# Gate products, decay sums and operand differences moved to VectorE, and mixer B started with its values

## The chip, the cores and the metric

The kernel runs on one core of one Trainium2 chip. The metric is the time on the device in microseconds (us). The kernel before takes 2028.79 us as the median of three runs (2027.69 to 2029.82).

A core has five engines with a queue of instructions each, worked off in order: TensorE (PE in the profile, its weight loads PEld), VectorE (DVE), ScalarE (ACT), GpSimd (POOL) and SyncE (SP), which here only starts transfers (DMA). An instruction that has to wait for another engine holds up everything behind it in its own queue.

## What is computed

The reference has two layers on a sequence of 512 tokens with 2048 features.

```
x: (1, 512, 2048) float32
# layer 1, mixer A (16 heads of 128)
h = rmsnorm(x);  q, fz, i, gate = split(h @ a_w_in)
log_f = logaddexp(log(lb), log1p(-lb) + log_sigmoid(fz))
k = (1 - lb) * sigmoid(-fz)
o = hgrn2_chunkwise(q, k, i, log_f)        # gated linear recurrence in chunks
x = x + (head_rmsnorm(o) * silu(gate)) @ a_w_out
# layer 2, mixer B (16 heads of 128)
h = rmsnorm(x);  k, v, f = split(h @ kv_w);  F = cumsum(log_sigmoid(f + bias))
q, gate = split(h' @ b_w_in)               # h' has its own norm weights
p = softmax(causal(head_rmsnorm(q) . head_rmsnorm(k) / sqrt(128) + F[t] - F[s]))
x = x + (head_rmsnorm(p @ v) * silu(gate)) @ b_w_out
```

`lb` is the lower bound of the forget gate, one number for each feature of the keys.

## The kernel before

Everything is kept with features on the 128 partitions and the 512 tokens along the free dimension: the stream is 16 tiles of 128 x 512. Each float32 operand of a large product is split in two (`split`, L439: a cast to a high part on ScalarE, L440, and the subtraction that gives the low part on VectorE, L441), and each product is made of three matmuls: high by high, high by low and low by high.

**Groups.** `group` (L220) is one pass over the 16 tiles of the stream with 512 output features in four PSUM banks, 192 matmuls of 512 columns. Its weights come from `Chunks` (L168): a transfer of 512 KB on SP's queue brings the weights of two steps into one of two `wr` buffers, and they are split into one of three `wh`, `wl` pairs. Where norm weights go into the weights, the split scales them (L147, L148), and for a group with two sets of scales it does so in two halves. Results are taken from the banks by an `evac` function: `qf_evac` (L544), `qk_evac` (L893), `v_evac` (L414) and `gate_evac` (L379).

**Mixers.** The order of the groups is written out by hand: `order_a` for mixer A, `order_b` for mixer B, with `q` for two heads of queries and keys (or forget inputs), `v` for four heads of values and `g` for the gates of four heads. After each `q` group two heads are added to a list of tasks, `mix_a` or `mix_b`, written as generators; `pump` takes steps from the list between the steps of the following groups, two a step in mixer A and one a step in mixer B. In mixer A GpSimd makes the logarithm of the decay (L568) and the small sums of it (L611 to L613, L661 to L663, L717, L718).

**Output projections.** `out_product` finishes all tasks, opens a new pool of buffers, and makes the first 512 features with a plain `group`, whose `before` splits the branch output (`y_split`) and, at every second step, prepares the operands for the rest (`quick_prep`, L254). The other 1536 features are six groups (`quick`, L270) in which a 2 x 2 block product takes seven products of half the columns in place of eight; the operand sums `m` of the stream come from `quick_prep`, those of the weights from `w_sums` (L153). Both take their buffers from the same two of the name `wm`. `w7h` and `w7l` are the split weights, in two buffers. `quick_sum` (L300) puts the products together and adds the residual, which a transfer has brought into one of four `z` buffers. The first projection's result `X1` is stored (`x1_done`, L809) for the residual of the second one, and kept. Its last quick group is only put together two steps into the first group of mixer B (`last_a`).

**Start of mixer B.** The first group of mixer B runs `x1_split` (L850) ahead of each of its 16 steps. It splits one tile of `X1` and adds its squares to a running sum (`norm1.add`, L349: a square on ScalarE, L354, into a `z` buffer, and a sum on VectorE, L355). After the last step the sum is finished, and the forget gate's product (`forget`) follows.

**The order on each engine.** The framework sorts the instructions of all engines by a timeline that it makes from its own costs, with the order of the program as priority; so the order in an engine's queue is fixed when the kernel is built, and it is not always that of the lines. Waits between engines are set by the framework from what each instruction reads and writes.

Of the kernel before, what the change touches and what calls it, by code (L numbers as in the profile page):

```python
# [12 lines left out]
AF = mybir.ActivationFunctionType  # L13
ALU = mybir.AluOpType
AX = mybir.AxisListType

P = 128
# [3 lines left out]
H = 16  # L21
# [5 lines left out]
RATE_A, RATE_B = 2, 1  # L27
# [5 lines left out]
def hgrn2_fox(ctx, tc, io):  # L33
# [24 lines left out]
    def const(tag, shape, dt=F32):  # L58
        return padded(cp, shape, dt, tag, tag)
# [108 lines left out]
    class Chunks:  # L168
# [33 lines left out]
        def split(self):  # L202
            if self.raw:
                fn, _ = self.raw.pop(0)
                self.parts.extend(fn())
# [47 lines left out]

    def quick_prep(p, y):  # L254

        k1, k2 = 2 * p, 2 * p + 1
        b11, b12, b21, b22 = y[k1][:, :TN], y[k1][:, TN:], y[k2][:, :TN], y[k2][:, TN:]
        m = mt("wm", (P, 4, TN), 2)
        V.tensor_sub(m[:, 0, :], b12, b11)
        G.tensor_sub(m[:, 2, :], b12, b22)  # L260
        V.tensor_sub(m[:, 1, :], b22, m[:, 0, :])
        V.tensor_sub(m[:, 3, :], b21, m[:, 1, :])
        th = mt(f"th{p}", (P, 3, TN), 1, F32R)
        tl = mt(f"tl{p}", (P, 3, TN), 1, F32R)
        split(m[:, 0, :], Xh[k1][:, TN:], Xl[k1][:, TN:])
        split(m[:, 1:4, :], th, tl)
        return th, tl

    def quick(banks, prep, evac, hold):

        half = lambda i: banks[i // 2][:, (i % 2) * TN : (i % 2 + 1) * TN]
        for p in range(KT // 2):
            if p % 2 == 0:
                wts.load()
            if not wts.parts:
                wts.split()
            h, l = wts.take()
            if not (wts.parts or hold and p == KT // 2 - 1):
                wts.split()
            th, tl = prep[p]  # L280
            k1, k2 = 2 * p, 2 * p + 1
            lo, hi = slice(0, TN), slice(TN, T)
            f, e = p == 0, p == KT // 2 - 1

            for i, (a, xh, xl) in enumerate((
                (2, Xh[k1][:, lo], Xl[k1][:, lo]),
                (5, th[:, 0, :], tl[:, 0, :]),
                (1, th[:, 2, :], tl[:, 2, :]),
                (3, Xh[k1][:, hi], Xl[k1][:, hi]),
                (0, Xh[k2][:, lo], Xl[k2][:, lo]),  # L290
                (6, Xh[k2][:, hi], Xl[k2][:, hi]),
                (4, th[:, 1, :], tl[:, 1, :]),
            )):
                o = half(i)
                PE.matmul(o, h[:, a, :], xh, start=f and i % 2 == 0, stop=False)
                PE.matmul(o, h[:, a, :], xl, start=False, stop=False)  # L296
                PE.matmul(o, l[:, a, :], xh, start=False, stop=e and (i % 2 == 1 or i == 6))
        return lambda: evac(*banks)
# [71 lines left out]
    def log_sigmoid(out, z, l):  # L370

        S.activation(l, z, AF.Abs)
        S.activation(l, l, AF.Exp, scale=-1.0)
        S.activation(l, l, AF.Ln, bias=1.0)
        V.scalar_tensor_tensor(out, z, 0.0, l, op0=ALU.min, op1=ALU.subtract)
# [3 lines left out]
    def gate_evac(norm, h0):  # L379
        def evac(j, bk):  # L380
            h = h0 + j
            new = Y[h] is None
            if new:
                Y[h] = nt(f"y{h}", (P, T), 1)
            z = Y[h] if new else nt("z", (P, T), 4)
            V.tensor_mul(z, bk, norm.row)
            l = tmp()
            log_sigmoid(l, z, l)
            S.activation(l, l, AF.Exp)
            G.tensor_mul(z, z, l)  # L390
            if not new:
                V.tensor_mul(Y[h], Y[h], z)

        return evac
# [92 lines left out]
    lb = const("lbv", (P, H))  # L487
    one_m = const("one_m", (P, H))
    log_lb = const("log_lb", (P, H))
    log_1m = const("log_1m", (P, H))  # L490
    diff = const("diff", (P, H))

    def lower_bounds():
        lbl = vec["lb"]
        V.tensor_sub(lb, lbl, lbl)
        S.activation(lb, lb, AF.Exp)
        V.reciprocal(one_m, lb)
        V.tensor_mul(lb, lb, one_m)
        V.tensor_sub(lb, lb, lb)
        S.activation(log_1m, lb, AF.Ln, scale=-1.0, bias=1.0)  # L500
        V.tensor_scalar(out=log_lb, in0=lb, scalar1=2.0**-60, scalar2=None, op0=ALU.max)
        S.activation(log_lb, log_lb, AF.Ln)
        V.tensor_scalar(out=one_m, in0=lb, scalar1=0.0, scalar2=NEG, op0=ALU.is_le, op1=ALU.mult)
        V.tensor_add(log_lb, log_lb, one_m)
        V.tensor_sub(diff, log_1m, log_lb)

    setup.append(lower_bounds)

# [35 lines left out]
    def qf_evac(h0):  # L544
        def evac(j, bk):
            h = h0 + j // 2
            need("qk", h - 3)
            need("g", h - 2)
            if j % 2 == 0:
                QA[h] = mt("q", (P, T), 3)  # L550
                V.tensor_mul(QA[h], bk, norm0.row)  # L551
                return
            z = nt("z", (P, T), 4)
            V.tensor_mul(z, bk, norm0.row)
            ls, l = tmp(), tmp()
            log_sigmoid(ls, z, l)
            V.scalar_tensor_tensor(l, z, 0.0, l, op0=ALU.max, op1=ALU.add)
            KA[h] = mt("k", (P, T), 3)
            b1 = log_1m[:, h : h + 1]
            S.activation(KA[h], l, AF.Exp, scale=-1.0, bias=b1)  # L560
            S.activation(l, ls, AF.Abs, bias=diff[:, h : h + 1])
            S.activation(l, l, AF.Exp, scale=-1.0)
            S.activation(l, l, AF.Ln, bias=1.0)
            V.tensor_scalar(
                out=ls, in0=ls, scalar1=b1, scalar2=log_lb[:, h : h + 1], op0=ALU.add, op1=ALU.max
            )
            GA[h] = mt("g", (P, T), 2)
            G.tensor_add(GA[h], ls, l)  # L568

        return evac  # L570

# [220 lines left out]
    norm1 = Norm()  # L792
    X1 = [None] * KT

    order_b = "q0 v0 q1 q2 v1 g0 q3 q4 v2 g1 q5 q6 v3 q7 g2 g3".split()
    nb, nk = vec["b_norm_w"], vec["kv_norm_w"]
    for name in order_b:
        ap = io[{"q": "wb_qk", "v": "wb_v", "g": "wb_g"}[name[0]]][int(name[1])]
# [9 lines left out]

    def x1_done(kt):  # L809
        nc.sync.dma_start(x1_d[kt], X1[kt])  # L810

    def out_a_evac():
        res = [res_a(j) for j in range(4)]
# [15 lines left out]
    def out_product(evac0, residual, evac, name, hold):  # L829

        flush()
        phase(name)
        prep = []

        def before(kt):
            y_split(kt)
            if kt % 2:
                prep.append(quick_prep(kt // 2, Yd))

        group(evac0, before=before)  # L840
        return quick_groups(prep, residual, evac, hold)
# [8 lines left out]
    def x1_split(kt):  # L850
        if kt == 2:
            last_a()
        if kt == 6:
            forget_weights()
        h, l = new_x(kt)
        split(X1[kt], h, l)
        norm1.add(X1[kt])
        X1[kt] = None
        if kt == KT - 1:
            norm1.finish()  # L860
# [14 lines left out]
    def forget():  # L875
        b = bank()
        for kt in range(KT):
            PE.matmul(b[0:48], wfs[:, kt, :], Xh[kt], start=kt == 0, stop=False)
            PE.matmul(b[0:48], wfs[:, kt, :], Xl[kt], start=False, stop=kt == KT - 1)
        z = nt("z", (P, T), 4)  # L880
        S.copy(z[0:H], b[32 : 32 + H])
        V.tensor_add(z[0:H], z[0:H], b[0:H])
        V.tensor_mul(z[0:H], z[0:H], norm1.row[0:H])
        V.tensor_scalar(out=z[0:H], in0=z[0:H], scalar1=vec["f_bias"], scalar2=None, op0=ALU.add)
        l = tmp()
        log_sigmoid(l[0:H], z[0:H], l[0:H])
        f = tmp()
        V.tensor_tensor_scan(f[0:H], l[0:H], l[0:H], initial=0.0, op0=ALU.add, op1=ALU.bypass)
        nc.sync.dma_start(f_d, f[0:H])
# [3 lines left out]
    def qk_evac(h0):  # L893
        def evac(j, bk):
            h = h0 + j % 2
            need("qk", h - 3)
            t = mt("q" if j < 2 else "k", (P, T), 3)
            (QB if j < 2 else KB)[h] = t
            V.tensor_mul(t, bk, norm1.row)

        return evac
# [78 lines left out]

    reached.clear()
    VV[:] = [None] * H
    first = True
    for name in order_b:
        kind, i = name[0], int(name[1])
        if kind == "q":
            group(qk_evac(2 * i), before=x1_split if first else None, rate=RATE_B)
            if first:
                forget()
            first = False  # L990
            tasks.append((2 * i, mix_b(2 * i)))
            tasks.append((2 * i + 1, mix_b(2 * i + 1)))
        elif kind == "v":
            group(v_evac(norm1, 4 * i), token_major=True, rate=RATE_B)
        else:
            group(gate_evac(norm1, 4 * i), rate=RATE_B, hold=name == order_b[-1])

    def res_b(kt):
        r = nt("z", (P, T), 4)
# [96 lines left out]
```

## Time and profile before

| | us |
|---|---|
| median of 3 runs | 2028.79 |
| profiled execution | 2028.22 |
| its span, first to last instruction | 2026.5 |
| TensorE busy | 1985.9 |
| VectorE busy | 1567.6 |
| ScalarE busy | 1129.0 |
| GpSimd busy | 271.9 |

The span is that of one execution, the rest of its time lies around it. In the rows of the profile, `out<-in` are the names of the tiles, `x1664` is a count, and the number in square brackets of a timeline row is how long the engine was idle just before it and what ended that. In groups of instructions, the first number after the bar is the busy time in us and the second the mean of one in ns. Instructions of one engine overlap at their ends, so that a row of 0.68 us can follow the one before it after 0.60.

Mixer A runs to about 860 us, the first output projection to about 1045, mixer B to about 1845, and the second projection to the end.

### The profile page before, as it was taken

To read this page: it belongs to the slowest core of one execution; us is meant where nothing else is said; L and a number is where in the kernel's file an instruction comes from. 1 tells how busy PE (TensorE), PEld (TensorE's weight loads), DVE (VectorE), ACT (ScalarE), POOL (GpSimd) and SP (SyncE) were. 2 spreads that over 40 slices of the span, in tenths; PEclk is the share of its full clock that TensorE was granted. 3 is DMA by queue.
4 is the path that set the end of the run, shared out by engine and by line. 5 is a ranking of instruction groups with operands and counts; after the bars stand their busy time and mean duration, and the time that the engine had idled before them with its cause. 6 is when DMAs were issued, how large, how long until landed. Compare 5 with 4: busy or idle time off the path is not lost.

```text
span 2026.5 us, 28907 instructions
## 1 busy us (share of the span) xinstructions
PE 1985.9 (98%) x10218; PEld 1697.4 (84%) x10218; DVE 1567.6 (77%) x3271; ACT 1129.0 (56%) x2312; POOL 271.9 (13%) x365
## 2 busy tenths in 40 slices
PE   9999999999999999989989999999999999999898
PEld 7888888888888888869977888888888888888898
DVE  7969977989799889798884667666766676687887
ACT  6646655666566466653363655554555556565432
POOL 3303211312133041130000000010001000012100
PEclk9999999999999999999999999999999999999899
DMA  5222222222222222335432232223223322323453
GB/s 188 83 84 73 73 84 83 74 81 76 80 78 70 77 84 73 94 113 166 151 99 91 92 95 92 88 81 104 92 80 97 96 86 87 91 81 107 138 162 104
DMA packets 61697, 195.02 MB, mean 96 GB/s; under 512 B 7904, under 2 KB 8032, under 8 KB 61552
## 3 DMA queue, kind: packets, MB, share of 16 engines
q1 hardware_dynamic: 61408, 193.17, 30.7%
q8 instruction: 80, 1.31, 0.3%
q14 instruction: 65, 0.53, 0.1%
q10 hardware_dynamic: 144, 0.01, 0.0%
HBM read 184.73 MB, written 8.42 MB: 95 GB/s over the span
## 4 chain that ended last, share of the span: by engine, by line
PE 71%; DVE 14%; DMA 6%; issue 3%; ACT 3%; POOL 3%; SPq 0%; DVEq 0%; ACTq 0%; POOLq 0%
PE gm L242 15%; PE gm L244 15%; PE gm L243 15%; PE gm L239 5%; PE gm L238 5%; PE gm L240 5%; DMA wr<-in_wb_q 3%; DVE wl L441 2%; DMA wr<-in_wa_q 2%; DVE w7l L441 2%; PE mx L587 1%; PE mx L585 1%; PE mx L586 1%; DVE ml L441 1%; PE mx L435 1%
## 5 line engine op out<-in xcount | busy, mean ns | idle before, releaser
L242 PE MATMUL gm<-xh,wh 128*128 128x512 f32 x1664 | 650.9, 392 | 4.0 <-ACT t L304 1.7
L243 PE MATMUL gm<-xl,wh 128*128 128x512 f32 x1664 | 650.2, 391 | 0.0
L244 PE MATMUL gm<-xh,wl 128*128 128x512 f32 x1664 | 613.2, 392 | 4.4 <-DVE wl L441 3.9
L242 PEld LDWEIGHTS gm<-xh,wh 128*128 128x128 f32 x1664 | 313.1, 188 | 68.6 <-ACT t L304 1.9
L244 PEld LDWEIGHTS gm<-xh,wl 128*128 128x128 f32 x1664 | 310.8, 188 | 69.6 <-DVE wl L441 7.2
L243 PEld LDWEIGHTS gm<-xl,wh 128*128 128x128 f32 x1664 | 313.1, 188 | 62.8
L441 DVE TENSOR_TENSOR wl<-wr,wh 128x512 fp32r<-128x512 f32 x288 | 213.2, 744 | 67.7 <-ACT wh L440 57.8
L440 ACT CAST wh<-wr 128x512 fp32r<-128x512 f32 x288 | 177.2, 619 | 124.1 <-PE gm L243 89.8
L148 DVE SCALAR_TENSOR_TENSOR wl<-wr,v_b_norm_w,wh 128x256 fp32r<-128x256 f32 (+1 forms) x192 | 113.1, 591 | 139.8 <-ACT wh L147 130.7
L147 ACT ACTIVATE wh<-wr,v_b_norm_w 128x256 fp32r<-128x256 f32 (+1 forms) x192 | 111.7, 585 | 186.2 <-PE gm L243 146.7
L239 PE MATMUL gm<-wl,xh 128*128 128x512 f32 x512 | 201.6, 394 | 0.4 <-DVE wl L441 0.4
L240 PE MATMUL gm<-wh,xl 128*128 128x512 f32 x512 | 199.9, 391 | 0.0
L238 PE MATMUL gm<-wh,xh 128*128 128x512 f32 x512 | 183.8, 392 | 0.3 <-DVE q L551 0.2
L147 ACT ACTIVATE wh<-wr,v_kv_norm_w 128x256 fp32r<-128x256 f32 (+1 forms) x192 | 110.3, 574 | 59.5 <-PE gm L240 43.2
L148 DVE SCALAR_TENSOR_TENSOR wl<-wr,v_kv_norm_w,wh 128x256 fp32r<-128x256 f32 (+1 forms) x192 | 111.2, 581 | 35.8 <-ACT wh L147 35.3
L938 POOL TENSOR_SCALAR_AFFINE_SELECT s<-s 128x128 f32<-128x128 f32 x64 | 27.4, 428 | 804.1 <-DVE s L937 803.5
L580 DVE COPY_PREDICATED at<-masks,mx 128x128 f32<-128x128 uint8 (+3 forms) x448 | 106.8, 297 | 11.2 <-PE mx L587 10.7
L238 PEld LDWEIGHTS gm<-wh,xh 128*128 128x128 f32 x512 | 96.0, 188 | 20.5 <-ACT wh L440 0.5
L239 PEld LDWEIGHTS gm<-wl,xh 128*128 128x128 f32 x512 | 96.3, 188 | 19.3 <-DVE wl L441 1.0
L240 PEld LDWEIGHTS gm<-wh,xl 128*128 128x128 f32 x512 | 96.3, 188 | 18.4
L440 ACT CAST w7h<-wr 128x768 fp32r<-128x768 f32 x48 | 40.1, 835 | 110.1 <-PE mx L296 45.3
L440 ACT CAST kh<-k 128x512 fp32r<-128x512 f32 (+1 forms) x96 | 56.4, 587 | 52.4 <-PE mx L586 19.4
(221 smaller groups left out, 3948.4 us busy)
## 6 DMA issues: line engine op xcount, KB each, us to landing
wr<-in_wb_qk SPq DMA_DIRECT2D x64, 512.0 KB, 3.5
wr<-in_wa_qf SPq DMA_DIRECT2D x62, 512.0 KB, 3.5
wr<-in_wa_v SPq DMA_DIRECT2D x32, 512.0 KB, 3.5
wr<-in_wa_g SPq DMA_DIRECT2D x32, 512.0 KB, 3.5
wr<-in_wb_v SPq DMA_DIRECT2D x32, 512.0 KB, 3.5
wr<-in_wb_g SPq DMA_DIRECT2D x32, 512.0 KB, 3.5
wr<-in_wa_q SPq DMA_DIRECT2D x24, 512.0 KB, 3.5
wr<-in_wb_q SPq DMA_DIRECT2D x24, 512.0 KB, 3.6
```

The lines of the kernel that those rows point to most:

```text
L147: S.activation(h[:, c], r[:, c], AF.Copy, scale=w[:, kt : kt + 1])
L148: V.scalar_tensor_tensor(l[:, c], r[:, c], w[:, kt : kt + 1], rd(h)[:, c], op0=ALU.mult, op1=ALU.subtract)
L238: PE.matmul(banks[j], xh, h, start=f, stop=False)
L239: PE.matmul(banks[j], xh, l, start=False, stop=False)
L240: PE.matmul(banks[j], xl, h, start=False, stop=e)
L242: PE.matmul(banks[j], h[:, c], Xh[kt], start=f, stop=False)
L243: PE.matmul(banks[j], h[:, c], Xl[kt], start=False, stop=False)
L244: PE.matmul(banks[j], l[:, c], Xh[kt], start=False, stop=e)
L440: S.copy(h, src)
L441: return V.tensor_sub(l, src, rd(h))
L580: V.copy_predicated(out, mv, data)
L938: G.affine_select(out=s[:, c], in_=s[:, c], pattern=[[-1, P]], compare_op=ALU.is_ge, fill=NEG, base=0, channel_multiplier=1,)
```

## The change

- In `gate_evac` the product of a gate's input with its sigmoid goes from GpSimd to VectorE.
- In `qf_evac` the factor 1 - lb goes into the logarithm (`Ln` of `c1 * e + c1` with `c1 = 1 / (1 - lb)`), so that `ls` holds the log sigmoid with log(1 - lb) already added; the sum that gives the log decay, on GpSimd before and with a VectorE step ahead of it, is one VectorE instruction. The setup makes `inv_1m` and `neg_lb` in place of `log_1m` and `diff`.
- In `quick_prep` one difference goes from GpSimd to VectorE, and the split of the first difference into `Xh`, `Xl` comes after the split of the other three; it is returned as a function, which `before` calls at once.
- `norm1.add` goes from `x1_split` to `x1_done`.
- Mixer B's order starts with `v0` and then `q0`; the first group, now `v0`, runs `x1_split` and is followed by `forget`.

The small sums of mixer A and the causal selection in mixer B (L938) stay on GpSimd.

```diff
     def quick_prep(p, y):
...
         V.tensor_sub(m[:, 0, :], b12, b11)
-        G.tensor_sub(m[:, 2, :], b12, b22)
+        V.tensor_sub(m[:, 2, :], b12, b22)
         V.tensor_sub(m[:, 1, :], b22, m[:, 0, :])
         V.tensor_sub(m[:, 3, :], b21, m[:, 1, :])
...
-        split(m[:, 0, :], Xh[k1][:, TN:], Xl[k1][:, TN:])
         split(m[:, 1:4, :], th, tl)
-        return th, tl
+        return th, tl, lambda: split(m[:, 0, :], Xh[k1][:, TN:], Xl[k1][:, TN:])
...
-            G.tensor_mul(z, z, l)
+            V.tensor_mul(z, z, l)
...
-        S.activation(log_1m, lb, AF.Ln, scale=-1.0, bias=1.0)
+        V.tensor_scalar(out=inv_1m, in0=lb, scalar1=-1.0, scalar2=1.0, op0=ALU.mult, op1=ALU.add)
+        V.reciprocal(inv_1m, inv_1m)
...
-        V.tensor_sub(diff, log_1m, log_lb)
+        V.tensor_scalar(out=neg_lb, in0=log_lb, scalar1=-1.0, scalar2=None, op0=ALU.mult)
...
-            log_sigmoid(ls, z, l)
+            c1, c2 = inv_1m[:, h : h + 1], log_lb[:, h : h + 1]
+            S.activation(l, z, AF.Abs)
+            S.activation(l, l, AF.Exp, scale=-1.0)
+            S.activation(l, l, AF.Ln, scale=c1, bias=c1)
+            V.scalar_tensor_tensor(ls, z, 0.0, l, op0=ALU.min, op1=ALU.subtract)
             V.scalar_tensor_tensor(l, z, 0.0, l, op0=ALU.max, op1=ALU.add)
...
-            S.activation(KA[h], l, AF.Exp, scale=-1.0, bias=b1)
-            S.activation(l, ls, AF.Abs, bias=diff[:, h : h + 1])
+            S.activation(KA[h], l, AF.Exp, scale=-1.0)
+            S.activation(l, ls, AF.Abs, bias=neg_lb[:, h : h + 1])
...
-            V.tensor_scalar(
-                out=ls, in0=ls, scalar1=b1, scalar2=log_lb[:, h : h + 1], op0=ALU.add, op1=ALU.max
-            )
-            G.tensor_add(GA[h], ls, l)
+            V.scalar_tensor_tensor(GA[h], ls, c2, l, op0=ALU.max, op1=ALU.add)
...
-    order_b = "q0 v0 q1 q2 v1 g0 q3 q4 v2 g1 q5 q6 v3 q7 g2 g3".split()
+    order_b = "v0 q0 q1 q2 v1 g0 q3 q4 v2 g1 q5 q6 v3 q7 g2 g3".split()
...
     def x1_done(kt):
         nc.sync.dma_start(x1_d[kt], X1[kt])
+        norm1.add(X1[kt])
...
                 prep.append(quick_prep(kt // 2, Yd))
+                prep[-1][2]()
...
         split(X1[kt], h, l)
-        norm1.add(X1[kt])
         X1[kt] = None
```

More of the change, by code (lines that the diff above doesn't have):

```diff
@@ L279, in quick @@
                 wts.split()
-            th, tl = prep[p]
+            th, tl, _ = prep[p]
             k1, k2 = 2 * p, 2 * p + 1
@@ L489, in hgrn2_fox @@
     log_lb = const("log_lb", (P, H))
-    log_1m = const("log_1m", (P, H))
-    diff = const("diff", (P, H))
+    neg_lb = const("neg_lb", (P, H))
+    inv_1m = const("inv_1m", (P, H))
     def lower_bounds():
@@ L555, in evac @@
             ls, l = tmp(), tmp()
-            log_sigmoid(ls, z, l)
+            c1, c2 = inv_1m[:, h : h + 1], log_lb[:, h : h + 1]
[3 more added lines that the diff above has]
+            V.scalar_tensor_tensor(ls, z, 0.0, l, op0=ALU.min, op1=ALU.subtract)
             V.scalar_tensor_tensor(l, z, 0.0, l, op0=ALU.max, op1=ALU.add)
             KA[h] = mt("k", (P, T), 3)
-            b1 = log_1m[:, h : h + 1]
-            S.activation(KA[h], l, AF.Exp, scale=-1.0, bias=b1)
-            S.activation(l, ls, AF.Abs, bias=diff[:, h : h + 1])
+            S.activation(KA[h], l, AF.Exp, scale=-1.0)
+            S.activation(l, ls, AF.Abs, bias=neg_lb[:, h : h + 1])
             S.activation(l, l, AF.Exp, scale=-1.0)
             S.activation(l, l, AF.Ln, bias=1.0)
-            V.tensor_scalar(
-                out=ls, in0=ls, scalar1=b1, scalar2=log_lb[:, h : h + 1], op0=ALU.add, op1=ALU.max
-            )
             GA[h] = mt("g", (P, T), 2)
-            G.tensor_add(GA[h], ls, l)
+            V.scalar_tensor_tensor(GA[h], ls, c2, l, op0=ALU.max, op1=ALU.add)
         return evac
@@ L982, in hgrn2_fox @@
     VV[:] = [None] * H
-    first = True
     for name in order_b:
         kind, i = name[0], int(name[1])
+        before = x1_split if name == order_b[0] else None
         if kind == "q":
[L987 to L990, printed above, removed]
+            group(qk_evac(2 * i), before=before, rate=RATE_B)
             tasks.append((2 * i, mix_b(2 * i)))
@@ L993, in hgrn2_fox @@
         elif kind == "v":
-            group(v_evac(norm1, 4 * i), token_major=True, rate=RATE_B)
+            group(v_evac(norm1, 4 * i), token_major=True, before=before, rate=RATE_B)
         else:
             group(gate_evac(norm1, 4 * i), rate=RATE_B, hold=name == order_b[-1])
+        if before:
+            forget()
     def res_b(kt):
```

## The prediction

> **What bounds the kernel now.** The order of reading was the first part of the page, then the busy time by stretches, then TensorE's own waits in the timeline.
>
> ```profile
> PE 1985.9 (98%) x10218; PEld 1697.4 (84%) x10218; DVE 1567.6 (77%) x3271; ACT 1129.0 (56%) x2312; POOL 271.9 (13%) x365
> 200.00:250.00 50.00, 49.15 (x245) 41.49 (x244) 49.08 (x126) 34.16 (x77) 10.91 (x15) 1.00 0.24 73
> 905.00:920.00 15.00, 9.56 (x59) 9.27 (x60) 11.50 (x19) 5.55 (x7) 0.00 (x0) 0.77 0.65 214
> 925.00:1015.00 90.00, 89.80 (x749) 89.60 (x748) 74.02 (x116) 35.69 (x41) 0.00 (x0) 1.00 0.48 153
> 1015.00:1055.00 40.00, 31.79 (x195) 28.55 (x194) 39.07 (x68) 25.95 (x49) 0.00 (x0) 0.91 0.24 83
> 1890.00:1905.00 15.00, 9.73 (x54) 9.43 (x54) 11.27 (x19) 4.95 (x7) 0.00 (x0) 0.66 0.65 211
> ```
>
> In the stretches the columns are the length, then busy time of PE, weight load, DVE, ACT and POOL, the granted clock, DMA share and GB/s. TensorE is busy for 98% and the change takes no matmul from it, so only its gaps can be won. They are bunched: at the start of the first output projection (905 to 920), at the start of mixer B (1015 to 1055) and at the start of the second output projection (1890 to 1905). In each the granted clock falls too: 15 x 0.23 = 3.45 us, 40 x 0.09 = 3.6 us and 15 x 0.34 = 5.1 us of full clock are lost. The waits themselves, in the PE timeline:
>
> ```profile
> 908.78 0.39 PE L295 MATMUL mx<-th,w7h 128*128 128x256 f32 x1 [4.04 <-ACT w7h L440]
> 912.17 0.58 PE L297 MATMUL mx<-th,w7l 128*128 128x256 f32 x1 [1.66 <-DVE w7l L441]
> ...
> 1025.85 0.39 PE L297 MATMUL gm<-xh,w7l 128*128 128x256 f32 x1 [1.20 <-DVE w7l L441]
> ...
> 1035.21 0.39 PE L295 MATMUL gm<-th,w7h 128*128 128x256 f32 x1 [3.39 <-ACT w7h L440]
> ...
> 1037.87 0.58 PE L297 MATMUL gm<-th,w7l 128*128 128x256 f32 x1 [0.81 <-DVE w7l L441]
> ...
> 1044.76 0.50 PE L242 MATMUL gm<-xh,wh 128*128 128x512 f32 x1 [1.68 <-ACT t L304]
> ...
> 1894.35 0.58 PE L295 MATMUL mx<-th,w7h 128*128 128x256 f32 x1 [4.34 <-ACT w7h L440]
> ...
> 1897.36 0.58 PE L297 MATMUL mx<-th,w7l 128*128 128x256 f32 x1 [0.93 <-DVE w7l L441]
> ```
>
> With the clock this makes 4.04 + 1.66 + 3.45 = 9.2 us, 1.20 + 3.39 + 0.81 + 1.68 + 3.6 = 10.7 us and 4.34 + 0.93 + 5.1 = 10.4 us: 30.3 us, all of it behind operands of the seven-product groups (`w7h`, `w7l`) that ScalarE and VectorE finish late. Mixer A adds one more group, from the waits of PE:
>
> ```profile
> PE mx L585 <- ACT mh L440: 4.9, 4, 1.6
> ```
>
> That is 4.9 us in four waits. Some 35 us in all is the most that can be won.
>
> **The change part by part: the two output projections.** Four gate products (L390) and eight differences (L260) leave GpSimd at each. What they do now, from the timelines of POOL, DVE and ACT at the first one:
>
> ```profile
> 863.82 6.36 POOL L390 TENSOR_TENSOR z<-z,t 128x512 f32<-128x512 f32 x4 [22.40 <-ACT t L389]
> 896.32 4.42 POOL L260 TENSOR_TENSOR wm<-y,y 128x256 f32<-128x256 f32 x2 [4.45 <-DVE tl L441]
> ...
> 862.15 0.69 DVE L375 SCALAR_TENSOR_TENSOR t<-z,t 128x512 f32<-128x512 f32 x1 [0.35 <-ACT t L374]
> ...
> 865.59 1.77 DVE L392 TENSOR_TENSOR y<-y,z 128x512 f32<-128x512 f32 x1
> 867.29 3.44 DVE L441 TENSOR_TENSOR wl<-wr,wh 128x512 fp32r<-128x512 f32 x2
> ...
> 872.95 0.68 DVE L392 TENSOR_TENSOR y<-y,z 128x512 f32<-128x512 f32 x1
> 875.36 0.75 DVE L259 TENSOR_TENSOR wm<-y 128x256 f32<-128x256 f32 x2
> ...
> 876.63 1.28 DVE L441 TENSOR_TENSOR wl<-wr,wh 128x512 fp32r<-128x512 f32 x2
> ...
> 900.06 0.96 DVE L261 TENSOR_TENSOR wm<-y,wm 128x256 f32<-128x256 f32 x1
> 900.95 0.41 DVE L262 TENSOR_TENSOR wm<-y,wm 128x256 f32<-128x256 f32 x1
> ...
> 907.23 0.42 DVE L158 TENSOR_TENSOR wm<-wm,wr 128x256 f32<-128x256 f32 x1
> ...
> 905.49 0.83 ACT L440 CAST w7h<-wr 128x768 fp32r<-128x768 f32 x1 [1.94 <-DMA wr<-in_wa_q]
> ...
> 907.68 1.04 ACT L440 CAST w7h<-wm 128x1024 fp32r<-128x1024 f32 x1 [1.05 <-DVE wm L158]
> ```
>
> The reader sees two costs of GpSimd. Its result is late: the last pair of L260 runs from 896.32 to 900.74 and L262 follows at 900.95. And VectorE is slowed beside it: the same L392 takes 1.77 us beside L390 and 0.68 after it, two `wl` 3.44 against 1.28, one L261 0.96 against the 0.41 of L262. The two `wm` buffers tie the rest together: L158, for the first weights of the quick groups, comes only after the operand sums have been split, and the cast of 907.68, which ends PE's wait, after L158.
>
> On VectorE the gates cost 4 x 0.61 = 2.4 us (0.68 with overlap: the two `wl` above step by 0.60) and the differences 8 x 0.34 = 2.7 us (L259 takes 0.75 for two, so 0.34 a step). Taken away are (1.77 - 0.68) + (3.44 - 1.28) + (0.96 - 0.41) = 3.8 us in the rows shown. So VectorE's work is close to even, and the bounds of this term are a chain 5.1 - 3.8 = 1.3 us later, if VectorE alone sets it, and one 4.42 - 0.75 + 3.8 - 2.4 = 5.1 us earlier, if the last pair's stay on POOL and the whole relief at the gates count. I take 3 us earlier, nearer the upper end, since the last gate result no longer waits for four products in a row and L262 no longer for POOL. The wait of 4.04 then falls to 1.0. Waits of 1.66 and 1.68 are not followed by a lower clock in the stretches, those of 3.39, 4.04 and 4.34 are, so the 3.45 us goes too: **6.5 us**. The second projection has the same shape: 4.34 falls to 1.3 and 5.1 us of clock returns: **8.1 us**. What is late next is the second weight chunk: its cast (905.49) waited for a load, and loads follow the `wl` splits.
>
> [...]
>
> The plain order inside `quick_prep` changes as well: the sums are cast and split before the first difference overwrites half of `Xh`. No instruction is added; the deferred part is called at once in the same step, so nothing leaves the plain group's loop. I count it at zero, between 0 and 0.41 us a pair (the step of one short instruction). Its cover is that the split half is read only by the quick groups.
>
> **The start of mixer B.** The 15 squares and sums of the norm move from here into the first projection.
>
> ```profile
> 1015.00:1055.00 40.00, 10.22 (x15) 0.91 0.24 83
> ...
> 1033.66 0.41 DVE L158 TENSOR_TENSOR wm<-wm,wr 128x256 f32<-128x256 f32 x1
> ...
> 1044.14 0.57 ACT L304 COPY t<-gm 128x512 f32<-128x512 f32 x1
> ...
> 1023.04 0.68 DVE L355 TENSOR_TENSOR rstd<-rstd,z 128x512 f32<-128x512 f32 x1
> ...
> 1032.27 0.68 DVE L355 TENSOR_TENSOR rstd<-rstd,z 128x512 f32<-128x512 f32 x1
> ```
>
> The first row is the stretch with L355 alone: 10.22 of the 39.07 us in which VectorE is full. Three of them (the first and the last shown, one between) stand ahead of L158 in its queue: 3 x 0.61 = 1.8 us. The 3.39 falls to 1.6, the clock (3.6) returns, and the copy L304, which stood behind squares on ScalarE, starts about 1.0 us earlier, for **6.4 us**; bounds 0 (the planner fills the freed places with splits of `X1`) and 10.7. Starting with `v0` adds no matmul; its weights are split whole and not in two halves, and the row totals of this stretch leave that under 1 us, counted at zero. Its cost if it went wrong is in the second mixing step: heads start one group later, 22 steps a pair at 16 steps a group, and both orders have caught up by `q3`. The forget gate's matmuls, its short chain and its one store on SP go with the first group, as before, now a group ahead of their first reader. The moved squares and sums issue no transfer.
>
> In the projection the sums fall on 925 to 1015, where VectorE has 16 us free of 90. Thirteen sums take 13 x 0.61 = 7.9 us of it, and ScalarE waits there for TensorE:
>
> ```profile
> ACT w7h L440 <- PE gm L296: 20.0, 8, 3.3
> ACT w7h L440 <- PE mx L296: 17.1, 8, 3.2
> ```
>
> 37.1 us in 16 waits, 2.3 us of slack each, cover a pair of squares (1.2 us). The squares take buffers of `z` that the residual loads use; those loads sit on SP's queue with the weights', already behind the stores that wait for the same result. I take **1 us lost** (bounds 0 and 7.9, with no cover).
>
> **Mixer A.** From the groups by line, and the chain:
>
> ```profile
> L568 POOL TENSOR_TENSOR g<-t,t 128x512 f32<-128x512 f32 x16 | 27.8, 1735 | 277.4 <-ACT t L563 272.0 <-DVE t L564 5.4
> L564 DVE TENSOR_SCALAR t<-t,log_1m,log_lb 128x512 f32<-128x512 f32 x16 | 9.2, 575 | 2.5 <-ACT t L561 2.5
> L557 DVE SCALAR_TENSOR_TENSOR t<-z,t 128x512 f32<-128x512 f32 x16 | 12.8, 799 | 0.2
> ```
>
> An addition of 1735 ns and a VectorE step of 575 become one like L557, 799 ns: 0.9 us earlier for the sums that start each head, 16 x 0.22 = 3.6 us more on VectorE. The small sums stay. ScalarE keeps seven functions a head, and the two more setup steps on VectorE are of 16 columns in the first group, well under the 575 ns of L564 each and once: zero. Of the 4.9 us I take **2 back**; bounds -5 and 4.9. Against it, the gate product now stands in VectorE's queue behind ScalarE's chain, with weight splits and score copies behind it: **1.5 us lost**, bounds 0 and 32 x 0.61 = 19.5.
>
> **Sum.** 6.5 + 8.1 + 6.4 + 2 - 1 - 1.5 = 20.5. One of the three clock drops I count as staying, since waits of 1.0 to 1.6 plus any delay come between 1.68 and 3.39, where no row says: 3.5 less. That is 17 us. The profiled execution took 2028.22 us (span 2026.5 and 1.7 around it), 0.57 under the median of the runs. 2028.2 - 17 = **2011**.
>
> [...]
>
> **The rivals.** *All waits go* (chance 0.15): the sums run early enough that no wait is left at all three places; 30.3 - 1 - 1.5 + 2 = 30 us, 1998. For it: the last gate product ended at 870.18 (863.82 + 6.36), and L392 behind it has room to come 3.8 us sooner by the rows above. Against: VectorE has 39.07 of 40 us filled. *VectorE stays the bound at both projections* (0.2): the 5.1 us added equals what the stretching cost, the waits stay, and only mixer B's start gains: 6.4 + 2 - 2.5 = 6, 2022. For it: 11.50 of 15 us busy even in the gap; against: the waits of L262 for POOL. *The change does nothing* (0.12): the planner's order keeps the casts behind the same loads (1.94 us at 905.49), 2027. *VectorE becomes the bound in mixer A* (0.08): the 16 gates of A stand in a queue that is at 49.08 of 50 us; each brings 0.61 us and a wait of 0.35 for its ScalarE input, as L375 has it at 862.15: 16 x 0.96 = 15.4, against nothing gained at the projections and 6 at B: 2028 + 15.4 - 6 = 2037. It decides once the steps of VectorE that 200 to 250 shows as full delay `mh` and `wl` more than the relief from GpSimd helps, that is above 1 us a gate. The forecast's own case has the remaining 0.45, from 2004 to 2018.
>
> **How the numbers follow.** About 0.2%, 4 us, is what can be told from no change. The forecast, the first two rivals and a little of the third are faster: 0.77; same 0.13; slower 0.10. The range takes in 1998 and 2022 with their own spread and leaves out the last rival: 1997 to 2028.
>
> **What would show it.** Right: no wait over 2 us before `w7h` at the three places, the granted clock there at 1.00 in at least two, no L390, L568 or L260 on POOL, L392 near 0.68 throughout, sums L355 between 910 and 1020. Wrong: the wait for `w7h` unchanged with VectorE full ahead of it, PE waits inside 925 to 1015, or PE busy under 49 of 50 in more stretches of mixer A.

## The result

The kernel after takes 2013.70 us, the median of four runs (2011.97 to 2014.79), against 2028.66 for the kernel before (2027.69 to 2029.82, here four runs). The ratio is 0.9929, with a 95% interval of 0.9917 to 0.9941: 15 us faster. The forecast was 2011 with a range of 1997 to 2028. The total came close, but by luck: most of the places from which it was to come did not, and the rest of this document is about that.

### The profile page after: what moved, and what is told of

Read it like the earlier page. It is cut to its first block, busy times and chain, and to the rows that moved or that the text cites. A ratio compares the mean times of both kernels' runs of the same rounds, so it can differ in the third digit from the quotient of the medians.

```text
span 2012.2 us, 28874 instructions
## 1 busy us (share of the span) xinstructions
PE 1978.6 (98%) x10218; PEld 1696.5 (84%) x10218; DVE 1558.8 (77%) x3321; ACT 1130.1 (56%) x2311; POOL 172.8 (9%) x301
## 4 chain that ended last, share of the span: by engine, by line
PE 84%; DVE 7%; DMA 4%; issue 2%; ACT 1%; POOL 1%; SPq 0%; DVEq 0%; ACTq 0%; POOLq 0%
PE gm L244 17%; PE gm L242 17%; PE gm L243 17%; PE gm L238 6%; PE gm L240 6%; PE gm L239 6%; DMA wr<-in_wb_q 2%; DVE w7l L441 2%; PE mx L590 2%; PE mx L589 2%; PE mx L588 1%; DMA wr<-in_wa_q 1%; PE mx L435 1%; PE mx L436 1%; PE mx L434 1%
## 5 line engine op out<-in xcount | busy, mean ns | idle before, releaser
L441 DVE TENSOR_TENSOR wl<-wr,wh 128x512 fp32r<-128x512 f32 x288 | 204.7, 714 | 66.8 <-ACT wh L440 56.8
L583 DVE COPY_PREDICATED at<-masks,mx 128x128 f32<-128x128 uint8 (+4 forms) x448 | 108.8, 297 | 13.4 <-PE mx L590 13.0
```

What stands on the lines that cost most here:

```text
L441: return V.tensor_sub(l, src, rd(h))
L583: V.copy_predicated(out, mv, data)
```

## The profile after

First the busy line of the page and the first lines of TensorE's waits (waiting line, releaser, us in total, times, longest).

```profile
PE 1978.6 (98%) x10218; PEld 1696.5 (84%) x10218; DVE 1558.8 (77%) x3321; ACT 1130.1 (56%) x2311; POOL 172.8 (9%) x301
```

```profile
PE mx L295 <- ACT w7h L440: 15.5, 2, 8.4
...
PE gm L244 <- DVE wl L441: 1.1, 2, 0.9
...
PE mx L588 <- ACT mh L440: 1.0, 3, 0.6
```

Ninety-nine us of work left GpSimd, and VectorE, which took most of it over, is 9 us less busy than before. The waits for `mh` in mixer A went from 4.9 us to 1.0. But the two long waits for `w7h`, which the change was to shorten, are now 15.5 us together, where they were 4.04 and 4.34. In the PE timeline:

```profile
902.99 0.58 PE L295 MATMUL mx<-th,w7h 128*128 128x256 f32 x1 [8.36 <-ACT w7h L440]
...
1019.40 0.58 PE L297 MATMUL gm<-th,w7l 128*128 128x256 f32 x1 [1.61 <-DVE w7l L441]
...
1879.07 0.58 PE L295 MATMUL mx<-th,w7h 128*128 128x256 f32 x1 [7.17 <-ACT w7h L440]
```

Waits alone don't say where the 14.3 us between the two spans went, since TensorE now comes to these places at other times. What does is the start of the first matmul of each group, in both traces. These are the rows after:

```profile
849.86 0.39 PE L242 MATMUL gm<-xh,wh 128*128 128x512 f32 x1
893.39 0.28 PE L295 MATMUL mx<-xh,w7h 128*128 128x256 f32 x1
923.50 0.28 PE L295 MATMUL gm<-xh,w7h 128*128 128x256 f32 x1
1004.19 0.28 PE L295 MATMUL gm<-xh,w7h 128*128 128x256 f32 x1
1030.71 0.40 PE L238 MATMUL gm<-wh,xh 128*128 128x512 f32 x1
1082.38 0.40 PE L242 MATMUL gm<-xh,wh 128*128 128x512 f32 x1
1826.91 0.39 PE L242 MATMUL gm<-xh,wh 128*128 128x512 f32 x1
1870.67 0.28 PE L295 MATMUL mx<-xh,w7h 128*128 128x256 f32 x1
1899.65 0.28 PE L295 MATMUL gm<-xh,w7h 128*128 128x256 f32 x1
```

The same matmuls of before start at 857.30, 903.51, 932.07, 1013.19, 1044.76, 1097.68, 1843.46, 1888.78 and 1917.81. The differences give the time of each stretch. A quick group without a wait takes 20.16 us in both traces.

| stretch | before | after | difference |
|---|---|---|---|
| mixer A, to the first projection | 857.30 | 849.86 | -7.4 |
| plain group and first quick group of it | 74.77 | 73.64 | -1.1 |
| quick groups 2 to 5 | 81.12 | 80.69 | -0.4 |
| last quick group and first group of mixer B | 84.49 | 78.19 | -6.3 |
| rest of mixer B | 745.78 | 744.53 | -1.3 |
| second projection: plain and first quick group | 74.35 | 72.74 | -1.6 |
| its quick groups 2 to 6 and the end | 108.69 | 112.55 | +3.9 |

So the first projection, from its plain group to the end of its first quick group, gained 1.1 us; the second one lost 2.3 over its length; and mixer A, which the forecast had as even, gained half of the total.

Why the first wait grew can be read from VectorE's queue after, with ScalarE's cast behind it:

```profile
889.35 0.42 DVE L260 TENSOR_TENSOR wm<-y 128x256 f32<-128x256 f32 x1
...
893.29 0.68 DVE L821 TENSOR_TENSOR y<-gm,z 128x512 f32<-128x512 f32 x1
...
894.23 1.88 DVE L821 TENSOR_TENSOR y<-gm,z 128x512 f32<-128x512 f32 x3
896.02 1.82 DVE L441 TENSOR_TENSOR tl<-wm,th 128x768 fp32r<-128x768 f32 x2
897.76 0.68 DVE L355 TENSOR_TENSOR rstd<-rstd,z 128x512 f32<-128x512 f32 x1
898.36 1.28 DVE L156 TENSOR_TENSOR wm<-wr 128x512 f32<-128x512 f32 x2
...
901.44 0.75 DVE L158 TENSOR_TENSOR wm<-wm,wr 128x256 f32<-128x256 f32 x2
```

```profile
884.56 0.84 ACT L440 CAST w7h<-wr 128x768 fp32r<-128x768 f32 x1 [1.11 <-DMA wr<-in_wa_q]
...
901.89 1.99 ACT L440 CAST w7h<-wm 128x1024 fp32r<-128x1024 f32 x2 [4.96 <-DVE wm L158]
```

The first weights of the quick groups had been loaded by 884.56. Their sums (L156 to L158) still come only at 898.36, behind the last two operand preparations (from 889.35 on), the four results of the plain group (L821) and one of the moved sums (L355), because the preparations hold both `wm` buffers. Two more moved sums stand between L156 and L158. The same row in the kernel before:

```profile
903.53 0.69 DVE L156 TENSOR_TENSOR wm<-wr 128x512 f32<-128x512 f32 x1
```

The sums are thus 5.2 us earlier, better than forecast; but TensorE is there at 893.39 instead of 903.51, 10.1 us earlier. The matmul that waits for the cast starts 5.8 us earlier than before (902.99 for 908.78), and 4.04 + 10.1 - 5.8 gives the new wait of 8.4.

## Experiments: parts of the change undone

The runs came in three sets, each beside the kernel before, whose median was 2028.67, 2028.11 and 2028.01 us; the ratios are to it. Where a time is set against the kernel after, that is against its 2013.70, taken in another set. Starts and lengths of groups are read from the first matmuls, as above. In some of the runs the framework also mixes the matmuls of two groups at their border; where that matters, it is said.

**Gates back on GpSimd.**

```diff
-            V.tensor_mul(z, z, l)
+            G.tensor_mul(z, z, l)
             if not new:
```

> The changed kernel with one part undone: the 32 gate products are on GpSimd again. Theory A (GpSimd's slow products stretch what VectorE does beside them and come late, and mixer A and the plain groups of the projections are where that shows): the 16 products of mixer A at 1.59 us each come back, mixer A is 5 to 8 us longer, the plain groups 2 us each, time 2020 to 2024. Rival B (the chain of the log decay sum is what mixer A gained): under 2 us longer, 2013 to 2016. Rival C (gates in VectorE's queue are a cost): shorter, under 2012.

Measured: 2019.82 us (2018.73 to 2020.79), ratio to before 0.9955 [0.9943, 0.9968]: 6.1 us more than after. The first quick matmul of the first projection starts at 898.24, 4.9 us later than after, although four matmuls of the plain group (0.9 us) now stand behind it. Of TensorE's waits, the one for the weights of the plain groups is the one that grew (after: 1.1 us in 2):

```profile
PE gm L244 <- DVE wl L441: 3.5, 3, 1.7
```

What follows: theory A holds in sign, and the time is just under its interval. Less of it lies in mixer A than expected: its 16 groups end at 853.67, 3.8 us later than after. Another 1.4 us lie in mixer B, which has the other half of the gates, and none in the second projection (185.1 us to the end for 185.3; its first quick group looks longer, 33.22 us for 28.98, but has 12 matmuls of the plain group in it). Of the parts undone one at a time, the gates cost the most. The groups of instructions show by how much the VectorE instruction behind a gate (L392) was lengthened; first with the gates back, then after.

```profile
L390 POOL TENSOR_TENSOR z<-z,t 128x512 f32<-128x512 f32 x32 | 46.5, 1461 | 212.9 <-ACT t L389 212.7
...
L392 DVE TENSOR_TENSOR y<-y,z 128x512 f32<-128x512 f32 x32 | 28.7, 896 | 2.4 <-POOL z L390 2.4
```

```profile
L392 DVE TENSOR_TENSOR y<-y,z 128x512 f32<-128x512 f32 x32 | 21.9, 686 | 0.1
L390 DVE TENSOR_TENSOR z<-z,t 128x512 f32<-128x512 f32 x32 | 21.7, 686 | 0.3
```

On VectorE a gate costs 686 ns, and 210 of them come back at once in L392. The move also changes the order that the framework makes of VectorE's queue; how much of the 6.1 us is lengthening and how much is order was not separated.

**Decay sum back in two instructions, one of them on GpSimd.**

```diff
-            V.scalar_tensor_tensor(GA[h], ls, c2, l, op0=ALU.max, op1=ALU.add)
+            V.tensor_scalar(out=ls, in0=ls, scalar1=c2, scalar2=None, op0=ALU.max)
+            G.tensor_add(GA[h], ls, l)
```

> The changed kernel with the log decay sum in two instructions again, a maximum on VectorE and a sum on GpSimd (16 of each; the logarithm keeps the folded factor). Theory A (gates): mixer A is 1 to 3 us longer, time 2014.5 to 2017. Rival B (the decay sum): mixer A is 5 us longer or more, 2019 to 2022.

Measured: 2016.52 us (2015.26 to 2019.18), ratio 0.9942 [0.993, 0.9955]: 2.8 us more than after, inside theory A's interval and under rival B's. The first quick matmul starts at 896.07, 2.7 us later than after, all of it from mixer A. (The profiled execution is the slowest of the five, 2019.18; what it has beyond that lies mostly at the last quick group ahead of mixer B, 29.14 us for 26.53, which the edit doesn't touch.) Here the wait for `mh`, the decayed keys, comes back (after: longest 0.6 us):

```profile
PE mx L589 <- ACT mh L440: 2.1, 2, 1.5
```

**Both back.** The two edits above together.

> The changed kernel with the gate products and the sum of the log decay both on GpSimd again. Undone alone each made mixer A 2.8 us longer (of the 7.4 us that the change took from it). If the two add up and nothing else acts there, mixer A is 5.6 us longer and the time 2020 to 2023; if they stand in for each other (either alone keeps GpSimd out of the way only in part), mixer A is 7 us longer or more, 2023 to 2027; if the rest of mixer A's gain has another source (the folded factor), mixer A stays 5 us or less longer.

Measured: 2020.98 us (2018.98 to 2024.12), ratio 0.9967 [0.9954, 0.998]: 7.3 us more than after, inside the first case's times; mixer A itself is 5.4 us longer, close to the first case's 5.6. The first quick matmul starts at 899.83, again with four matmuls of the plain group behind it: 6.4 us later than after, where the two alone made 4.9 + 2.7 = 7.6. Before it was 903.51. With the 0.9 us of the four matmuls, gates and decay sum account for 7.3 of the 10.1 us by which TensorE comes earlier to the quick groups. Some 2.8 us are left for what else was changed up to there, the folded factor in the logarithm and the order it gives, the preparation's differences and its later split. They were not tried one by one, except the differences:

**One difference of each preparation back on GpSimd.**

```diff
-        V.tensor_sub(m[:, 2, :], b12, b22)
+        G.tensor_sub(m[:, 2, :], b12, b22)
```

> The changed kernel with one difference of each operand preparation back on GpSimd (16 in all). If VectorE's amount of work sets the waits of 8.4 and 7.2 us for w7h, taking 16 x 0.34 us from it shortens each by 1 to 3 us, or leaves the time as it is where GpSimd's stretching takes the same back: 2010 to 2014. If the lateness of the GpSimd result was the cost, as the forecast had it, each wait grows by 1 to 3 us: 2016 to 2020.

Measured: 2013.22 us (2010.52 to 2015.82), ratio 0.9922 [0.9908, 0.9936], no difference from after (2013.70), as the first case had it. The wait stays as it was:

```profile
902.69 0.58 PE L295 MATMUL mx<-th,w7h 128*128 128x256 f32 x1 [8.02 <-ACT w7h L440]
```

This goes against the forecast's reading that L262 waiting for GpSimd was part of what made `w7h` late.

**Norm sums back at the start of mixer B.**

> The changed kernel with the squares and sums of the norm back at the start of mixer B. If they were in the way there (forecast 6.4 us for it, less 1 us in the projection): the first group of mixer B is 4 to 6 us longer and the quick groups of the first projection 0 to 1 us shorter, time 2017 to 2020. If their place is hidden in both (rival): 2013 to 2015.

```diff
         nc.sync.dma_start(x1_d[kt], X1[kt])
-        norm1.add(X1[kt])
...
         split(X1[kt], h, l)
+        norm1.add(X1[kt])
         X1[kt] = None
```

Measured: 2017.06 us (2016.35 to 2018.16), ratio 0.9941 [0.9929, 0.9954]: 3.4 us more than after, at the low end of the first case. The place is as expected: last quick group and first group of mixer B take 84.35 us for 78.19 after, so the whole of the 6.2 us comes back, with the wait of before (3.39) almost to the digit:

```profile
PE gm L295 <- ACT w7h L440: 3.3, 1, 3.3
```

Against it the first quick group is 1.3 us shorter (28.77 for 30.11) without the sums in it, and the second projection is 1.7 us shorter (133.59 for 135.28 from its first quick matmul to its last), for which the sums do nothing; the second projection's share moves by such amounts in several of the runs.

**Queries first again.**

```diff
-    order_b = "v0 q0 q1 q2 v1 g0 q3 q4 v2 g1 q5 q6 v3 q7 g2 g3".split()
+    order_b = "q0 v0 q1 q2 v1 g0 q3 q4 v2 g1 q5 q6 v3 q7 g2 g3".split()
```

> The changed kernel with mixer B's order as before, q0 and then v0. The forecast counted the order at zero: 2012 to 2015, with mixer B's groups adding up to the same. Rival: the values first are part of why the start of mixer B got shorter (their weights are split whole), and without them it is 2 to 3 us longer, 2015.5 to 2017.

Measured: 2014.74 us (2014.07 to 2016.37), ratio 0.9936 [0.9922, 0.995]. All of mixer B takes 796.35 us for 796.19, so its groups add up to the same, as forecast. The rival's 2 to 3 us can be found, in the last quick group and the first group of mixer B together (80.72 us for 78.19), but the same stretch took 81.05 with the decay sum back, an edit that leaves it alone, so they can't be put down to the order. The last quick group ahead of it is 2.3 us longer (28.82 for 26.53), and the quick groups of the second projection 2.6 us shorter; the total of 1.0 us can't be told from none.

## Experiments: the order in VectorE's queue

The theory after the first four runs, called D: what keeps `w7h` late is neither GpSimd nor VectorE's amount of work, but that the last two preparations stand ahead of the first weight sums and hold the `wm` buffers. Steps 6 and 7 of a quick group are the first that need these preparations. So they can be made inside it:

```diff
         def before(kt):
             y_split(kt)
-            if kt % 2:
+            if kt % 2 and kt < 12:
                 prep.append(quick_prep(kt // 2, Yd))
                 prep[-1][2]()
...
     def quick(banks, prep, evac, hold):
...
+            if p in (2, 4) and len(prep) < 8:
+                prep.append(quick_prep(len(prep), Yd))
+                prep[-1][2]()
             th, tl, _ = prep[p]
```

> The changed kernel with the last two operand preparations of each projection (steps 12 to 15 of the plain group) moved into the first quick group, ahead of its steps 2 and 4; nothing is added or left out. In VectorE's queue 18 instructions then stand behind the first two pairs of weight sums (L156, L158) and no longer ahead of them. Theory D (the waits of 8.4 and 7.2 us for w7h come from that order, with the two wm buffers): both waits fall under 2 us, VectorE stays full to about 905 and then has room, time 1999 to 2005. Rival E (VectorE's amount of work is the bound, the place doesn't matter): the waits turn up again within the first quick group, before later products, time 2011 to 2015.

> As late, but the two preparations stand ahead of steps 1 and 3 of the first quick group. Theory D: the first weight sums come just as early, so the same first waits, and the time is within 2 us of late; a difference over 3 us would mean that the place inside the quick group matters, so that VectorE's work there and not only its order is the limit.

Measured: 2003.48 us (2001.22 to 2005.32), ratio 0.988 [0.9864, 0.9896], ahead of steps 2 and 4; 2000.02 us (1997.78 to 2000.78), ratio 0.986 [0.9847, 0.9874], ahead of steps 1 and 3. That is 10.2 and 13.7 us less than after. With steps 1 and 3, VectorE's queue and TensorE's waits:

```profile
888.87 0.69 DVE L156 TENSOR_TENSOR wm<-wr 128x512 f32<-128x512 f32 x1
...
892.36 0.42 DVE L158 TENSOR_TENSOR wm<-wm,wr 128x256 f32<-128x256 f32 x1
...
894.49 0.42 DVE L158 TENSOR_TENSOR wm<-wm,wr 128x256 f32<-128x256 f32 x1
```

```profile
PE gm L300 <- DVE w7l L444: 4.6, 6, 1.6
...
PE gm L298 <- ACT w7h L443: 1.4, 2, 0.7
```

The sums start at 888.87 in place of 898.36, no wait for `w7h` is longer than 0.7 us, and the first 168 matmuls of the quick groups, as many as one group has, take 23.03 and 22.21 us for 30.11 and 28.98 (the framework here mixes the first two groups). Theory D holds, rival E falls: 14 us hung on the order alone. The expectation that the two places would be within 2 us failed; they differ by 3.5. Of the 4.9 between the two profiled spans, 3.4 lie behind the second projection's first quick matmul. By the bar set there the place inside the quick group counts too. VectorE is indeed full for a while there:

```profile
896.00:910.00 14.00, 13.30 (x111) 13.30 (x112) 13.40 (x25) 5.17 (x8) 0.00 (x0) 1.00 0.56 189
```

**Ahead of steps 0 and 2.**

```diff
-            if p in (1, 3) and len(prep) < 8:
+            if p in (0, 2) and len(prep) < 8:
```

> As late13, with the two preparations ahead of steps 0 and 2. Steps 1 and 3 took 3.5 us less than 2 and 4. If earlier is better as long as the first chunk's sums come first, 1997 to 2000; if the second chunk's sums now stand behind a preparation, as in early, a wait of 1 to 3 us for them comes back in each projection, 2001 to 2006.

Measured: 2001.38 us (1999.05 to 2003.63), ratio 0.9869 [0.9855, 0.9883], at the edge of its second case. A wait for `w7h` of up to 2.0 us is back, as that case had it; the 1.4 us to steps 1 and 3 are too little to call one place better.

**The first chunk's sums alone earlier.** A function of `Chunks`, called at step 13 of the plain group, makes the first quick chunk's split ahead of the preparation of that step; the preparations stay in the plain group.

```diff
     class Chunks:
+        def early(self):
+            i = next(i for i, (_, n) in enumerate(self.raw) if n == 2)
+            done = self.raw[i][0]()
+            self.raw[i] = (lambda: done, 2)
...
             y_split(kt)
+            if kt == 13:
+                wts.early()
```

> The changed kernel with the weight sums and splits of the first quick chunk emitted one step earlier than the preparations that end the plain group (at its step 13), so that 16 fewer instructions stand ahead of them on VectorE; nothing else moves. Theory D: the first wait for w7h falls under 3 us, but the second chunk's sums still stand behind both preparations, so a wait for the second chunk of 2 to 5 us takes a part of its place: 2005 to 2010. Rival E: 2011 to 2015.

Measured: 2005.48 us (2004.27 to 2007.33), ratio 0.989 [0.9877, 0.9904], in theory D's interval. There is no wait for the first chunk's `w7h`; the longest is 3.2 us, for the second chunk, whose sums still stand behind both preparations, as expected:

```profile
PE mx L300 <- ACT w7h L445: 4.7, 2, 3.2
```

**The same order in the kernel before.** The edit with steps 1 and 3, made to the kernel before and nothing else, asks whether the waits of 4.04 and 4.34 us there had been GpSimd's.

> The kernel before with one edit alone: the last two operand preparations of each projection stand in the first quick group, ahead of its steps 1 and 3. The forecast put the waits of 4.04 and 4.34 us there down to GpSimd (late differences, stretched VectorE work). If that was right, this edit takes little of them: 2024 to 2029. Theory D (the order in VectorE's queue, the two wm buffers): both waits fall under 2 us although GpSimd still makes gates and differences, and the time falls by 8 to 14 us, 2014 to 2020.

Measured: 2019.70 us (2017.69 to 2021.09), ratio 0.9957 [0.9944, 0.997]: 8.3 us faster than before with all of GpSimd's work where it was. The waits for `w7h` at the two projections are gone but for 1.9 us, and that at the start of mixer B (3.4), which the edit doesn't touch, is still there:

```profile
PE gm L297 <- ACT w7h L442: 3.4, 1, 3.4
...
PE mx L297 <- ACT w7h L442: 1.9, 2, 1.4
```

**The better order, with one difference on GpSimd.** Steps 1 and 3, and in `quick_prep`:

```diff
-        V.tensor_sub(m[:, 2, :], b12, b22)
+        G.tensor_sub(m[:, 2, :], b12, b22)
```

> late13 with one difference of each preparation back on GpSimd. With the order mended VectorE is still full from 896 to 910 (13.40 of 14 us) and 16 x 0.34 us could leave it; if its amount of work is what is left, 1997 to 1999.5; if GpSimd's results and stretching take it back, as in the run with the differences back alone, 1999 to 2002.

Measured: 2007.20 us (2006.31 to 2007.84), ratio 0.9896 [0.988, 0.9912]: 7.2 us more than without it, outside both cases. In VectorE's queue the framework now puts a preparation between the weight sums, and the second L158 comes at 898.80 where it was 894.49, and at the second projection at 1874.49 where it was 1865.69; the waits for `w7h` are back:

```profile
894.20 0.41 DVE L260 TENSOR_TENSOR wm<-y 128x256 f32<-128x256 f32 x1
...
898.80 0.41 DVE L158 TENSOR_TENSOR wm<-wm,wr 128x256 f32<-128x256 f32 x1
...
1869.28 0.69 DVE L156 TENSOR_TENSOR wm<-wr 128x512 f32<-128x512 f32 x1 [2.05 <-DMA wr<-in_wb_q]
...
1874.49 0.42 DVE L158 TENSOR_TENSOR wm<-wm,wr 128x256 f32<-128x256 f32 x1
```

```profile
PE mx L298 <- ACT w7h L443: 7.5, 4, 3.2
PE gm L298 <- ACT w7h L443: 3.9, 1, 3.9
```

So the part of the change that was worth nothing by itself is worth 7 us once the order is mended. Of the 10.1 us between the two profiled spans only 0.7 have come up by the third quick group of the first projection; 1.9 lie at the start of mixer B, where the wait of 3.9 stands, and 7.4 in the second projection. The rows show a changed order, and a load that VectorE waits for; whether GpSimd's own time adds to it was not separated.

## Why the prediction was right in the total and wrong in its parts

| step of the forecast | forecast, us | measured, us |
|---|---|---|
| first projection's start | 6.5 won | 1.1 won |
| second projection | 8.1 won | 2.3 lost |
| start of mixer B | 6.4 won | 6.3 won |
| mixer A, with the gates in VectorE's queue | 2 - 1.5 = 0.5 won | 7.4 won |
| quick stage, moved norm sums | 1 lost | 0.4 won; 1.3 lost in the first quick group |
| order of mixer B | 0 | 1.3 won in the rest of mixer B, none by the run without it |
| one clock drop staying | 3.5 lost | all three stayed, inside the rows above |

**The projections** are where it failed, in the step "I take 3 us earlier ... The wait of 4.04 then falls to 1.0". The chain on VectorE did come earlier, by 5.2 us, which is the upper end of its bounds. But the step set the moved chain against a TensorE that stays where it was. TensorE came 10.1 us earlier, since mixer A (7.4) and the plain group (2.7) gained too, and the wait grew to 8.36. The price was too high as well. The first quick groups took 28.56 and 29.03 us before, 8.4 and 8.9 more than a group without a wait, where the forecast had 9.2 and 10.4 for waits and clock: half clock that falls on a wait was counted twice. The cause behind it was misread as well: the difference on GpSimd cost nothing there (2013.22 without that edit), and the order of preparations and weight sums in VectorE's queue was the bound before and after, as 8.3 and 13.7 us from that one edit show. The forecast had the row for it, L158 "only after the operand sums have been split", and named the two `wm` buffers, but took the order as given and counted only what was ahead in the queue. The rival "VectorE stays the bound at both projections" was the right one for these two places, though by the order of VectorE's work and not by its amount.

At the second projection the first wait of 7.17 did cost no more than before (72.74 us against 74.35 with the plain group), but the quick groups 2 and 3 took 22.91 and 22.07 us in place of 20.16. There VectorE waits for weights:

```profile
1897.68 0.69 DVE L156 TENSOR_TENSOR wm<-wr 128x512 f32<-128x512 f32 x1 [3.07 <-DMA wr<-in_wb_q]
...
1915.91 0.69 DVE L156 TENSOR_TENSOR wm<-wr 128x512 f32<-128x512 f32 x1 [3.90 <-DMA wr<-in_wb_q]
```

No term of the sum had this, though the forecast named a load as what would be late next. Why the loads are late there stays open; no run was made for it.

**The start of mixer B** was right in its mechanism and its size: 6.3 us came, and the run with the sums put back gave 6.2 of them back. Two terms inside it were off against each other: the clock did not return to full (0.91 over 40 us, as before, so none of the 3.6 came), and the waits shrank from 1.20 + 3.39 + 0.81 + 1.68 = 7.1 us to 1.07 + 1.61 = 2.7, by 4.4 where 1.8 and 1.0 were forecast. With the smaller waits TensorE was idle for 8.2 of 40 us before and 2.9 after, 5.3 less; the last 1.0 of the 6.3 us stays open.

**Mixer A** was mis-sized: 2 us back and 1.5 lost were forecast, 7.4 won. TensorE's idle time up to the first projection fell from 10.8 us to 5.8. The waits for `mh`, the term taken at 2, gave 3.9 of that. The term for the gates had the wrong sign: the forecast counted their relief of VectorE at the projections alone, and in mixer A only their place in its queue as a cost, but with the gates back on GpSimd mixer A is 3.8 us longer, and with the decay sum back 2.7. The rival in which 16 gates make VectorE the bound of mixer A fell: with the gates back on GpSimd the time rose.

**The moved sums** fall less than forecast on 925 to 1015, 5.49 us in 8 instructions, and TensorE has no wait there; the 15 sums run from 897.8 to 1036.3 and not between 910 and 1020:

```profile
925.00:1015.00 90.00, 5.49 (x8) 1.00 0.46 151
```

Of what the forecast named as signs, no L390, L568 or L260 on POOL and L392 at 0.69 came true; "no wait over 2 us before `w7h`" and "the granted clock there at 1.00 in at least two" of the three places did not. The sign listed as wrong, a wait for `w7h` with VectorE full ahead of it, is what the trace shows. The total was met by luck, because mixer A's 6.9 us more and the projections' 15.8 us less (14.6 forecast, 1.2 lost) stand against each other, with 3.5 set aside for the clock and 2.7 from the quick stage and the rest of mixer B: 17 - 15.8 + 6.9 + 3.5 + 2.7 = 14.3, less 0.1 at the start of mixer B.

## What to carry to other kernels

A wait is the distance between two chains; when a change moves both, work out when the waiting engine arrives as well as when its operand is ready. Where an operand is late, look first at what stands ahead of it in its engine's queue and could stand behind: an edit of the order alone was worth 8 us in the kernel before and 14 in the one after, as much as the whole change. A part that is worth nothing by itself can be worth 7 us after the bound is moved, so the undoing of parts is to be repeated then.

## What the runs showed of the hardware

In these traces the length of a wait alone does not tell whether TensorE's granted clock falls. In the kernel after it is at half from 1018.68 to 1025.51, from within the second of two waits of only 1.07 and 1.61 us. In the run with steps 1 and 3 and one difference on GpSimd, the matmuls behind a wait of 3.23 us take 0.28 us a row, as ahead of it; at half clock the same rows take 0.41 (kernel after, from 903.58 to 905.72).

```profile
1876.04 0.38 PE L298 MATMUL mx<-th,w7h 128*128 128x256 f32 x1 [3.23 <-ACT w7h L443]
1876.27 0.28 PE L299 MATMUL mx<-tl,w7h 128*128 128x256 f32 x1
1876.38 0.28 PE L298 MATMUL mx<-xh,w7h 128*128 128x256 f32 x1
```

The changes of the granted clock in the kernel after come at 899.22, 906.04, 1018.68, 1025.51, 1875.43 and 1882.25. The times between them, 6.83, 112.64, 6.83, 849.92 and 6.83 us, are 2, 33, 2, 249 and 2 steps of 3.413 us, the largest step that fits all five. The stretches that follow are laid on such steps (length, PE, PEld, DVE, ACT and POOL busy, clock, DMA share, GB/s). First the kernel before, the stretch ahead of each of its falls at the two projections and at the start of mixer B:

```profile
905.81:909.22 3.41, 0.44 (x3) 0.44 (x4) 2.86 (x6) 2.35 (x4) 0.00 (x0) 1.00 0.13 20
1032.10:1035.51 3.41, 0.30 (x2) 0.30 (x3) 3.41 (x9) 2.32 (x4) 0.00 (x0) 1.00 0.11 13
1888.85:1892.26 3.41, 1.16 (x10) 0.96 (x8) 2.49 (x5) 0.88 (x2) 0.00 (x0) 1.00 0.33 129
```

TensorE is busy for 0.13, 0.09 and 0.34 of them. Ahead of the falls in the kernel after it is not busy at all at the two projections (895.80 to 899.22 and 1872.02 to 1875.43, inside the waits of 8.36 and 7.17 us), and for 0.42 at the start of mixer B:

```profile
1015.27:1018.68 3.41, 1.45 (x10) 1.13 (x9) 3.41 (x6) 1.26 (x3) 0.00 (x0) 1.00 0.70 236
1018.68:1022.10 3.42, 2.70 (x12) 2.70 (x13) 3.42 (x6) 2.00 (x4) 0.00 (x0) 0.50 0.20 78
```

And at the second projection with the preparations ahead of steps 2 and 4, then 1 and 3, each with a wait of 1.56 us:

```profile
1866.06:1869.48 3.42, 1.79 (x13) 1.39 (x12) 3.42 (x7) 1.75 (x2) 0.00 (x0) 1.00 0.69 202
1869.48:1872.89 3.41, 3.29 (x15) 3.30 (x16) 3.41 (x9) 0.40 (x1) 0.00 (x0) 0.50 1.04 391
```

```profile
1865.86:1869.27 3.41, 1.84 (x15) 1.64 (x15) 3.41 (x6) 1.04 (x1) 0.00 (x0) 1.00 0.98 358
1869.27:1872.68 3.41, 3.41 (x31) 3.41 (x30) 3.35 (x9) 1.97 (x4) 0.00 (x0) 1.00 1.03 380
```

1.45 of 3.41 (0.42) and 1.79 of 3.42 (0.52) are followed by half the clock, 1.84 of 3.41 (0.54) is not. But no busy share parts the cases: in the kernel before, a stretch of 0.51 right behind one at half clock is followed by the full clock, and so is one of 0.47 in the run with steps 1 and 3 and one difference on GpSimd, which holds 1.81 us of the wait of 3.23 above:

```profile
1042.34:1045.75 3.41, 1.73 (x10) 1.40 (x10) 3.09 (x6) 2.27 (x5) 0.00 (x0) 1.00 0.00 0
1045.75:1049.17 3.42, 2.54 (x11) 1.78 (x10) 3.42 (x8) 0.63 (x1) 0.00 (x0) 1.00 0.00 0
```

```profile
1871.20:1874.62 3.42, 1.61 (x14) 1.40 (x12) 3.42 (x8) 0.00 (x0) 0.00 (x0) 1.00 0.38 145
```

No run set the share by itself, and what makes the clock fall is not shown. The forecast sorted waits by their length, with a limit between 1.68 and 3.39 us; the waits of 1.07 and 1.61 us with half the clock lie under it, and no length parts them from the one of 3.23 us without. And the drop during the long wait cost little: the first quick group after takes 30.11 us, 9.95 more than 20.16, of which the wait is 8.36, so the 6.8 us at half clock (899.22 to 906.04) cost 1.6; 3.8 of them lie on the wait itself.
